# A conformer layer's normed rows in PSUM, its second half's squares on GpSimd, another order of its first projection, and three edits further on

## Chip, cores and metric

The kernel runs on one core of a Trainium2 chip. The metric is device time in microseconds (us) of one execution. All inputs and outputs lie in HBM, in fp32.

## What is computed

A decoder trunk of two layers over 1024 positions of width 1024, cut to what the change touches:

```python
def conformer_conv(u, b_glu, w_dw, b_dw, ln_g, ln_b):
    u = u + b_glu
    a, gate = jnp.split(u, 2, axis=-1)
    v = a * jax.nn.sigmoid(gate)
    v = causal_dwconv(v, w_dw, b_dw)          # width 31, 768 channels
    v = layernorm(v, ln_g, ln_b)
    return jax.nn.silu(v)

# layer 0
h = rmsnorm(x, g_mix[0])
mem_k, mem_v = jnp.split(rmsnorm(mem, g_mem) @ w_mem_kv[0], 2, axis=-1)
p = h @ w_in_a[0]                             # [gate and value | memory queries]
mix = conformer_conv(p[..., :1536], ...)
x = x + concat(mix, memory_attention(p[..., 1536:], mem_k, mem_v)) @ w_out[0]
x = x + conv_ffn(rmsnorm(x, g_ffn[0]), ...)
# layer 1
kvf = rmsnorm(x, g_kv) @ w_kvf                # k, v, 12 forget logits
cum_logf = cumsum(log_sigmoid(kvf[..., 1536:] + b_f))
# queries, forgetting attention with bias cum_logf, memory attention,
# output projection, conv_ffn, final rmsnorm
```

## The kernel before

The sequence lies along the free axis: x is held as eight tiles of 128 channels x 1024 positions, and nearly every step is done for each half of 512 positions (hf 0 and 1). A product in fp32 is made of three fp32r matmuls (lines 108 to 110): each operand is split into a high part, copied by ScalarE (line 81), and a low part, the source minus the high part, on VectorE or GpSimd (line 82). So each tile that TensorE uses needs one copy and one subtract ahead of it.

TensorE, VectorE, ScalarE and GpSimd each run their own queue in order, and wait at an instruction whose operand or buffer isn't ready. A scheduler sets the order within each queue from the order of the program and its own estimates; `issue_after(ins)` holds an instruction behind another one, `later(d)` lowers its priority, and `set_fill` with `drain_fill(n)` doles out a list of steps, n of them at once.

**Start of layer 0** (`layer_a`). `normed(hf)` takes the sum of squares of x over channels (squares on ScalarE, line 152; adds at line 157, and at 159 where two accumulators are joined), sums over partitions with a matmul by ones (line 133), takes the root (line 140, ScalarE) and its reciprocal (line 142, VectorE), and spreads the result over the partitions with four matmuls by the identity (line 123). Those write the first half of the PSUM tile xn (tag b2, two banks). For each of the eight tiles line 801 then makes x * gain * row in an SBUF tile ppre, and line 802 splits it to ah and al. ALO lists the (hf, k) whose subtract runs on GpSimd; TWO = 5 starts a second accumulator for the second half's squares, whose adds run on VectorE. The sum in the first half of positions is psq, in the second nsq. Between these stand the memory's projections mk (line 108 to 110) and mv (line 222) of layer 1 and then layer 0, with the steps on their results, ks and vs.

**Projection and convolution.** The columns of w_in_a come in 128-wide tiles: wia0 to wia5 values (ua), wia6 to wia11 gates (ug), wia12 and 13 memory queries (uq). A step adds two of eight channel tiles for one half. For each channel tile t the order is gate hf 0, gate hf 1, value hf 0, value hf 1, in PSUM banks c0 and c1 by hf. v is value times sigmoid(gate). The depthwise convolution of width 31 is shared out: some taps are diagonal matmuls on TensorE into cpe (lines 108 to 110), some are a ScalarE product ct and a GpSimd add into yp (lines 874 and 875), the rest run on VectorE, in place in cpe for tiles 0 to 4 (line 918). The last tile, v5, is done by half, and its VectorE taps go to an SBUF accumulator (lines 886 and 888) that line 889 adds to yp; line 914 adds yp and cpe. The LayerNorm takes its mean by matmul (line 1014, bank c0 for hf 0, c1 for hf 1) and subtracts it at line 1019. Memory attention runs beside this (ms scores, line 230 and 265 amp, line 276 mt, lines 280 and 281 mo, om its output projection).

**Layer 1** (`layer_b`). The statistics of x are st (line 133) and bc (line 123). The value projection vps (line 1122) takes 24 matmuls for each of eight blocks of 128 positions, three times over, in banks c0 and c1 in turn. Keys and queries (pq) are made by half in bank c0 or c1 and multiplied by the row of the norm into bkc (line 1181) or bqc (line 1183), which sets the bank free. The forget logits are transposed (lft, blf) and summed along the positions by a scan (line 1215, VectorE); line 1218 copies the high part and line 1219 subtracts it. Scores are fs (line 1260).

Of the kernel before, what the change touches and what calls it, by code (L numbers as in the profile page):

```python
# [8 lines left out]
F32 = mybir.dt.float32  # L9
# [3 lines left out]
ALU = mybir.AluOpType  # L13
AX = mybir.AxisListType

P = 128
S = 1024
HS = 512
D = 1024
KD = D // P  # L20
# [31 lines left out]
class Trunk:  # L52
# [668 lines left out]
    def layer_a(self):  # L721
# [14 lines left out]
        with tc.tile_pool(name="pm", bufs=1) as pm:  # L736
# [23 lines left out]
            def ptmp(nm, w=HS):  # L760
                return pm.tile([P, HS], F32, tag="t", name=f"p{nm}", bufs=4)[:, :w]
# [24 lines left out]

            hh, hl = [], []

            def normed(hf):
                xs = [self.x[k][:, hf * HS:(hf + 1) * HS] for k in range(KD)]  # L790
                acc = self.sum_squares(xs, tmp=None if hf else ptmp, eng=nc.gpsimd if hf else nc.vector,
                                       two=self.TWO if hf else None)
                tmp = self.ps.tile([P, 2, HS], F32, tag="b2", name="xn")
                row = self.bcast_row(self.rstd_cols(acc, 4, D, self.eps_rms, tmp[:, 1, :4]), 4, tmp[:, 0])
                hh.append([])
                hl.append([])
                for k in range(KD):
                    hh[hf].append(self.htile(f"ah{hf}{k}"))
                    hl[hf].append(self.htile(f"al{hf}{k}"))
                    t = ptmp("pre")  # L800
                    nc.vector.scalar_tensor_tensor(t, xs[k], self.vec("g_mix0", k), row, op0=ALU.mult, op1=ALU.mult)
                    self.split(hh[hf][k], hl[hf][k], t, lo_eng=nc.gpsimd if (hf, k) in self.ALO else nc.vector)

# [7 lines left out]
            last_bc = self.last_bc.ins  # L811
            normed(0)
            normed(1)
            wv1 = [f(pm2) for f in wv1]
# [7 lines left out]
            self.ps.ring = ("c2", "c3")  # L822
            self.mem_v(mh, ml, rc, vs0, wv0)

            wk0 = [f(pm2) for f in wk0]
            ks0 = tuple(unit([P, NMH, MEM], F32R, f"ks0{i}") for i in range(2))
            self.mem_k(mh, ml, mrb, ks0, wk0)
            self.ps.ring = ("c0", "c1", "c2", "c3")
            nc.sync.dma_start(self.d_ks[0], ks1[0].bitcast(F32))
# [12 lines left out]
        wtl = pb.tile([P, CT * CW], F32R, tag="wtl", name="wtl")  # L842
        self.split(wth, wtl, self.vec("w_dwa", 0, CT * CW))

# [8 lines left out]
        def conv_steps(t):  # L853
# [9 lines left out]
            def start():  # L863
# [12 lines left out]
                if last:  # L876

                    with self.later(self.LATER):
                        d["a"] = []
                        for hf in range(2):  # L880
                            a = self.nt("ca")
                            d["a"].append(a)
                            for j in range(np_, CW):
                                vj = v[:, hf * HS + j:hf * HS + j + HS]
                                if j == np_:
                                    nc.vector.tensor_scalar(a, vj, w(j), None, op0=ALU.mult)
                                else:
                                    nc.vector.scalar_tensor_tensor(a, vj, w(j), a, op0=ALU.mult, op1=ALU.add)
                            nc.vector.tensor_tensor(y[:, hf], y[:, hf], a, op=ALU.add)
# [51 lines left out]
        def glu_steps(t):  # L941
# [3 lines left out]
            def step(i):  # L945
                val, hf, kk = i // 8, i // 4 % 2, i % 4
                j = t if val else CT + t
                if i % 8 == 0:
                    load(j)
                    for j2 in order[order.index(j) + 1:order.index(j) + 2]:  # L950
                        load(j2)
                if kk == 0:
                    d["u"] = self.ps.tile([P, HS], F32, tag=f"c{hf}", name="ua" if val else "ug")
                half(ws[j], d["u"], hf, [2 * kk, 2 * kk + 1])
# [22 lines left out]
        self.set_fill(steps + cv[CT - 1]["taps"], self.ARATE, self.ALAG)  # L977
        self.drain_fill(self.AFIRST)
        memattn(0)
# [65 lines left out]
    def layer_b(self):  # L1045
# [60 lines left out]
        def v_steps(pc_):  # L1106
# [3 lines left out]
            def step(i):  # L1110
# [4 lines left out]
                if kk == 0:  # L1115
                    d["ps"] = self.ps.tile([P, VP], F32, tag=f"c{t % 2}", name="vps")
                ps = d["ps"]
# [47 lines left out]
        def kq_steps(t):  # L1165
# [3 lines left out]
            def step(i):  # L1169
# [9 lines left out]
                if k == KD - 1:  # L1179
                    if n == "k":  # L1180
                        nc.vector.tensor_tensor(d[n][:, sl], d["u"], rb[:, sl], op=ALU.mult)
                    else:
                        nc.vector.scalar_tensor_tensor(d[n][:, sl], d["u"], SCALE, rb[:, sl],
                                                       op0=ALU.mult, op1=ALU.mult)
# [29 lines left out]
        cum = unit([NFOX, S], F32, "cum")  # L1214
        nc.vector.tensor_tensor_scan(cum, on, lf, 0.0, op0=ALU.mult, op1=ALU.add)
        ch = unit([NFOX, S], F32R, "ch")
# [90 lines left out]

        self.drain_fill(self.AHEAD)
        vss = {(0, 0): prep(0, 0), (0, 1): prep(0, 1)}
# [112 lines left out]
    MLAG = 3  # L1422
    ALO = [(0, 3), (0, 4), (0, 6), (1, 1), (1, 3), (1, 4)]
    TWO = 5
    WEARLY = 0
# [154 lines left out]
```

## Time and profile before

| | us |
|---|---|
| median of 3 runs | 2335.38 |
| lowest and highest | 2333.52, 2335.58 |
| the profiled execution's own time | 2334.59 |
| its span on the core | 2332.8 |

The mean granted clock of TensorE was 0.988 of full speed. Times in the rows of the profile are counted from the start of the span. A row of the time line gives start, duration, engine, line, operation, output <- inputs, shape and count; what stands in brackets is the idle time ahead of it and what ended it. A row of the waits gives who waited for whom, the total, how often, and the longest. The rows that the prediction uses are quoted there.

### The profile page before, as it was taken

What the parts mean: (1) busy time and instruction counts of PE and PEld (TensorE: products, weight loads), DVE (VectorE), ACT (ScalarE), POOL (GpSimd) and SP (SyncE); (2) the same over time, 40 slices, a digit from 0 to 9 for tenths busy, and PEclk for the clock granted to TensorE, in tenths of its full rate; (3) what the DMA queues carried; (4) which work ended last, traced back from release to release, by engine and by line L of the source; (5) the groups of instructions that cost most, each with busy time, mean ns of one, the idle gap of its engine ahead of it and who ended that gap; (6) DMA issues with size and microseconds to landing.
All of it is one profiled execution on the core that took longest, in us unless ns stands there. A gap on an engine that the chain in (4) does not pass through costs nothing.

```text
span 2332.8 us, 29689 instructions
## 1 busy us (share of the span) xinstructions
PE 2256.2 (97%) x10970; PEld 1865.7 (80%) x10970; DVE 1460.0 (63%) x1995; ACT 1075.5 (46%) x1864; POOL 1333.7 (57%) x1003
## 2 busy tenths in 40 slices
PE   6999889999999999999998999999999999999998
PEld 6777668878788878888897888788878888778887
DVE  7479787676666664325656777876776666645225
ACT  6776746443434343223542666755444343442212
POOL 3676844666868676453323443614577777766533
PEclk8999989999999999999999999999999999999999
DMA  6100023222222235332332222433222222245322
GB/s 242 37 28 28 29 73 117 72 81 82 82 76 88 78 108 188 106 109 95 123 105 81 71 77 68 124 110 127 67 86 75 81 75 88 79 136 175 112 68 73
DMA packets 85282, 216.74 MB, mean 93 GB/s; under 512 B 9009, under 2 KB 29233, under 8 KB 85137
## 3 DMA queue, kind: packets, MB, share of 16 engines
q1 hardware_dynamic: 84992, 214.52, 28.8%
q8 instruction: 86, 1.41, 0.3%
q14 instruction: 60, 0.48, 0.1%
q10 hardware_dynamic: 144, 0.32, 0.0%
HBM read 156.94 MB, written 51.58 MB: 89 GB/s over the span
## 4 chain that ended last, share of the span: by engine, by line
PE 46%; DVE 3%; POOL 1%; ACT 1%; issue 1%; DMA 0%; DVEq 0%; ACTq 0%; POOLq 0%
PE uY L345 8%; PE uX L345 5%; PE uV L345 5%; PE dn L109 3%; PE dn L108 3%; PE dn L110 3%; PE vps L1122 3%; PE pq L108 2%; PE pq L110 2%; PE pq L109 2%; PE op L108 1%; PE op L109 1%; PE op L110 1%; PE fo L1305 1%; PE fs L1260 1%; PE fo L1304 1%
## 5 line engine op out<-in xcount | busy, mean ns | idle before, releaser
L345 PE MATMUL uY<-fT,fwh 128*128 128x512 f32 x1056 | 331.4, 395 | 4.7 <-DVE fuv L546 3.2
L109 PE MATMUL dn<-gl,wd_hi 128*128 128x512 f32 (+1 forms) x752 | 284.6, 379 | 1.2 <-POOL gl L82 1.2
L108 PE MATMUL dn<-gh,wd_hi 128*128 128x512 f32 (+1 forms) x752 | 280.3, 377 | 0.0
L662 DVE TENSOR_TENSOR fx<-fx,dn 128x512 f32<-128x512 f32 (+1 forms) x176 | 110.9, 636 | 268.8 <-PE dn L110 268.5
L110 PE MATMUL dn<-gh,wd_lo 128*128 128x512 f32 (+1 forms) x752 | 278.9, 375 | 0.0
L345 PEld LDWEIGHTS uY<-fT,fwh 128*128 128x128 f32 x1056 | 196.3, 188 | 55.3 <-DVE fuv L546 9.8
L345 PE MATMUL uX<-fB,fwh 128*128 128x512 f32 x704 | 220.0, 393 | 2.0 <-ACT fuv L521 1.9
L345 PE MATMUL uY<-fT,fwl 128*128 128x512 f32 x528 | 206.6, 391 | 0.0
L82 POOL TENSOR_TENSOR fwl<-wa,fwh 128x512 fp32r<-128x512 f32 x88 | 117.1, 1331 | 137.6 <-ACT fwh L81 137.5
L82 POOL TENSOR_TENSOR wd_lo<-wd_raw,wd_hi 128x1024 fp32r<-128x1024 f32 x44 | 107.9, 2458 | 137.8 <-ACT wd_hi L81 129.0
L108 PEld LDWEIGHTS dn<-gh,wd_hi 128*128 128x128 f32 x752 | 141.2, 188 | 28.3
L109 PEld LDWEIGHTS dn<-gl,wd_hi 128*128 128x128 f32 x752 | 141.3, 188 | 27.0 <-POOL gl L82 2.0
L110 PEld LDWEIGHTS dn<-gh,wd_lo 128*128 128x128 f32 x752 | 141.0, 188 | 27.1
L345 PEld LDWEIGHTS uX<-fB,fwh 128*128 128x128 f32 x704 | 131.6, 188 | 33.3 <-ACT fuv L521 2.8
L82 POOL TENSOR_TENSOR fwl<-wb,fwh 128x512 fp32r<-128x512 f32 x88 | 121.9, 1387 | 63.1 <-ACT fwh L81 60.8
L875 POOL TENSOR_TENSOR yp<-yp,ct 128x512 f32<-128x512 f32 x100 | 135.7, 1359 | 27.6 <-ACT ct L874 22.7
L82 POOL TENSOR_TENSOR gl<-g,gh 128x512 fp32r<-128x512 f32 x88 | 117.5, 1357 | 47.1 <-ACT gh L81 47.1
L345 PE MATMUL uX<-fB,fwl 128*128 128x512 f32 x352 | 137.3, 392 | 0.0
L82 POOL TENSOR_TENSOR fwl<-fs,fwh 128x512 fp32r<-128x512 f32 x88 | 117.8, 1340 | 20.1 <-ACT fwh L81 20.1
L81 ACT CAST fwh<-wa 128x512 fp32r<-128x512 f32 x88 | 54.2, 618 | 140.7 <-PE uY L345 108.3
L81 ACT CAST wd_hi<-wd_raw 128x1024 fp32r<-128x1024 f32 x44 | 45.6, 1050 | 157.6 <-issue 82.2
L345 PEld LDWEIGHTS uY<-fT,fwl 128*128 128x128 f32 x528 | 99.2, 188 | 22.3
(398 smaller groups left out, 6285.4 us busy)
## 6 DMA issues: line engine op xcount, KB each, us to landing
wb<-in_wup SPq DMA_DIRECT2D x44, 512.0 KB
wa<-in_wup SPq DMA_DIRECT2D x44, 512.0 KB
d_g<-fsg SPq DMA_DIRECT2D x44, 512.0 KB
wd_raw<-in_wdn SPq DMA_DIRECT2D x44, 512.0 KB
g<-d_g SPq DMA_DIRECT2D x44, 512.0 KB
d_x<-x SPq DMA_DIRECT2D x32, 256.0 KB
nxs<-d_x SPq DMA_DIRECT2D x32, 256.0 KB
wia_raw<-in_wia SPq DMA_DIRECT2D x14, 512.0 KB
```

The costliest lines, as they stand in the source:

```text
L81: nc.scalar.copy(hi, src)
L82: (lo_eng or nc.gpsimd).tensor_tensor(lo, src, hi.bitcast(F32), op=ALU.subtract)
L108: nc.tensor.matmul(out, lhsT=ah, rhs=bh, start=start and i == 0, stop=False)
L109: nc.tensor.matmul(out, lhsT=ah, rhs=bl, start=False, stop=False)
L110: nc.tensor.matmul(out, lhsT=al, rhs=bh, start=False, stop=stop and i == n - 1)
L345: mm = nc.tensor.matmul(out, lhsT=w[:, k], rhs=h[k], start=start and k == 0 and j == 0, stop=k == n - 1 and j == 2, skip_group_check=True)
L662: return nc.vector.tensor_tensor(self.x[m][:, sl], self.x[m][:, sl], ps, op=ALU.add)
L875: nc.gpsimd.tensor_tensor(y[:, hf], y[:, hf], c, op=ALU.add)
L1122: nc.tensor.matmul(ps, lhsT=a[hf][k][:, tsl], rhs=w[:, k % 4], start=k == 0 and j == 0, stop=k == KD - 1 and j == 2)
L1260: mm = nc.tensor.matmul(o, lhsT=d["q1"][:, qs], rhs=d["k1"][:, ksl], start=True, stop=False)
L1304: nc.tensor.matmul(po, lhsT=vs[:, j], rhs=ph[:, u], start=j == 0, stop=False)
L1305: nc.tensor.matmul(po, lhsT=vs[:, j], rhs=pl[:, u], start=False, stop=j == 2 * I + 1)
```

## The change

Part 1, the start of layer 0. The product x * gain * row goes to the free banks of the two xn tiles, two slots for the first half of positions and three for the second, except for the three tiles whose subtract runs on GpSimd, which keep the SBUF tile. ALO shrinks from six entries to three, TWO goes, so that all seven adds of the second half's squares are GpSimd's. `normed` is cut in two, the statistics and the rows; the memory's value projection of layer 0 is held behind the first half's broadcast, and the second half's rows come after the memory's key projection of layer 0.

Part 2, the projection. For t = 0 the order is gate and value of hf 0, then gate and value of hf 1, and all but two of its first steps are held behind the second half's broadcast.

Part 3, further on: the last tile's accumulator ca lies in PSUM (bank c0 and c1) instead of SBUF; the first two vps tiles use banks c2 and c3; eight steps of keys are issued ahead of the scan, which is held behind the last bkc among them.

```diff
-            def normed(hf):
-                xs = [self.x[k][:, hf * HS:(hf + 1) * HS] for k in range(KD)]
-                acc = self.sum_squares(xs, tmp=None if hf else ptmp, eng=nc.gpsimd if hf else nc.vector,
-                                       two=self.TWO if hf else None)
-                tmp = self.ps.tile([P, 2, HS], F32, tag="b2", name="xn")
-                row = self.bcast_row(self.rstd_cols(acc, 4, D, self.eps_rms, tmp[:, 1, :4]), 4, tmp[:, 0])
+            rows = [self.ps.tile([P, 2, HS], F32, tag="b2", name="xn") for hf in range(2)]
...
+            def squares(hf):
+                return self.sum_squares(xs2[hf], tmp=None if hf else ptmp, eng=nc.gpsimd if hf else nc.vector)
+            def stats(hf):
+                tmp = rows[hf]
+                r = self.rstd_cols(squares(hf), 4, D, self.eps_rms, tmp[:, 1, :4])
+                return self.bcast_row(r, 4, tmp[:, 0])
+            def normed(hf, row):
...
-                    t = ptmp("pre")
+                    if (hf, k) in self.ALO:
+                        t = ptmp("pre")
+                    else:
+                        t = (rows[hf][:, 1], rows[1 - hf][:, 0], rows[0][:, 1])[n % (2 + hf)]
+                        n += 1
                     nc.vector.scalar_tensor_tensor(t, xs[k], self.vec("g_mix0", k), row, op0=ALU.mult, op1=ALU.mult)
-                    self.split(hh[hf][k], hl[hf][k], t, lo_eng=nc.gpsimd if (hf, k) in self.ALO else nc.vector)
+                    e = nc.scalar.copy(hh[hf][k], t)
+                    (nc.gpsimd if (hf, k) in self.ALO else nc.vector).tensor_tensor(
+                        hl[hf][k], t, hh[hf][k].bitcast(F32), op=ALU.subtract)
+                return e.ins
...
-            normed(0)
-            normed(1)
+            row0 = stats(0)
+            bc0 = self.last_bc.ins
+            normed(0, row0)
+            row1 = stats(1)
+            bc1 = self.last_bc.ins
...
-            self.mem_v(mh, ml, rc, vs0, wv0)
-            wk0 = [f(pm2) for f in wk0]
+            with tc.issue_after(bc0):
+                self.mem_v(mh, ml, rc, vs0, wv0)
+                wk0 = [f(pm2) for f in wk0]
...
             self.mem_k(mh, ml, mrb, ks0, wk0)
+            last_ah = normed(1, row1)
...
-        self.split(wth, wtl, self.vec("w_dwa", 0, CT * CW))
+        with self.issue_after(last_ah):
+            self.split(wth, wtl, self.vec("w_dwa", 0, CT * CW))
...
-                            a = self.nt("ca")
+                            a = self.ps.tile([P, HS], F32, tag=f"c{hf}", name="ca")
...
-                val, hf, kk = i // 8, i // 4 % 2, i % 4
+                val, hf, kk = (i // 8, i // 4 % 2, i % 4) if t else (i // 4 % 2, i // 8, i % 4)
...
-                    d["u"] = self.ps.tile([P, HS], F32, tag=f"c{hf}", name="ua" if val else "ug")
+                    d["u"] = self.ps.tile([P, HS], F32, tag=f"c{hf if t else val}", name="ua" if val else "ug")
...
-        self.drain_fill(self.AFIRST)
+        self.drain_fill(2)
+        with self.issue_after(bc1):
+            self.drain_fill(self.AFIRST - 2)
...
-                    d["ps"] = self.ps.tile([P, VP], F32, tag=f"c{t % 2}", name="vps")
+                    d["ps"] = self.ps.tile([P, VP], F32, tag=f"c{t % 2 + 2 * (t < 2 and pc_ == 0)}", name="vps")
...
-                        nc.vector.tensor_tensor(d[n][:, sl], d["u"], rb[:, sl], op=ALU.mult)
+                        self.last_k = nc.vector.tensor_tensor(d[n][:, sl], d["u"], rb[:, sl], op=ALU.mult)
...
-        nc.vector.tensor_tensor_scan(cum, on, lf, 0.0, op0=ALU.mult, op1=ALU.add)
+        self.drain_fill(8)
+        with self.issue_after(self.last_k.ins):
+            nc.vector.tensor_tensor_scan(cum, on, lf, 0.0, op0=ALU.mult, op1=ALU.add)
...
-        self.drain_fill(self.AHEAD)
+        self.drain_fill(self.AHEAD - 8)
...
-    ALO = [(0, 3), (0, 4), (0, 6), (1, 1), (1, 3), (1, 4)]
-    TWO = 5
+    ALO = [(1, 1), (1, 3), (1, 5)]
```

On TensorE's queue, at the start of layer 0, where the first half's statistics (psq) are followed by the 48 mv matmuls of layer 0's memory values:

```order
 L222 MATMUL mv<-mwkl,mh 128x256
 L133 MATMUL xn<-ones_69,psq 128x1 x4
+L123 MATMUL xn<-ident,rs 128x128 x4
 L222 MATMUL mv<-mwwh,mh 128x256
 L222 MATMUL mv<-mwwh,ml 128x256
```

The broadcast (line 123), which stood behind the 48 mv, now stands ahead of them, directly behind the statistics. After them come 2 ug, 24 mk, 7 ug, 24 mk and 3 ug ahead of the second half's statistics, then its broadcast, then 12 ug, 24 ua, 24 uq, 24 uq, 24 ug and 24 ua; on GpSimd four of the seven adds of squares come first, then one wia_lo ahead of each of the other three.

On VectorE's queue at the same place, where rs is the first half's reciprocal, ppre or xn the product and al the low part (line 801 became 814, the subtract of line 82 became 816):

```order
 L142 RECIPROCAL rs<-sd 128x4
-L226 SCALAR_TENSOR_TENSOR vs_542<-mv,rs,vs_542 128x4x64
 L784 CAST maskb<-nmask 128x128
-L226 SCALAR_TENSOR_TENSOR vs_542<-mv,rs,vs_542 128x4x64
-L801 SCALAR_TENSOR_TENSOR ppre<-x_90,vecs,xn 128x512
-L801 SCALAR_TENSOR_TENSOR ppre<-x_91,vecs,xn 128x512
-L801 SCALAR_TENSOR_TENSOR ppre<-x_92,vecs,xn 128x512
-L801 SCALAR_TENSOR_TENSOR ppre<-x_93,vecs,xn 128x512
-L82 TENSOR_TENSOR al_262<-ppre,ah_261 128x512
+L814 SCALAR_TENSOR_TENSOR xn<-x_90,vecs,xn 128x512
+L816 TENSOR_TENSOR al_263<-xn,ah_262 128x512
+L814 SCALAR_TENSOR_TENSOR xn<-x_91,vecs,xn 128x512
```

Products and subtracts of the first half now alternate, since the products have two slots, and the adds of squares that stood among them are gone from this queue.

On VectorE's queue in layer 1, around the scan (printed with operation SCALAR_TENSOR_TENSOR; lines 1211, 1181, 1215 and 1219 became 1234, 1204, 1241 and 1245):

```order
-L1211 COPY blf<-lft 12x512
-L1215 SCALAR_TENSOR_TENSOR bcum<-bon,blf 12x1024
-L1219 TENSOR_TENSOR bcl<-bcum,bch 12x1024
-L1181 TENSOR_TENSOR bkc<-pq,rb 128x512 x2
-L1267 TENSOR_REDUCE nm<-fs 128x1 x2
+L1234 COPY blf<-lft 12x512
+L1204 TENSOR_TENSOR bkc<-pq,rb 128x512
+L1241 SCALAR_TENSOR_TENSOR bcum<-bon,blf 12x1024
+L1245 TENSOR_TENSOR bcl<-bcum,bch 12x1024
+L1204 TENSOR_TENSOR bkc<-pq,rb 128x512
```

The first of the two bkc now stands ahead of the scan. Of the other two edits, the mean matmuls of the convolution's first four tiles (line 1014) leave their places ahead of mt (hf 0) and beside cpe of hf 1, and stand behind cpe of hf 0 and behind the second group of om; and 24 vps stand between st (line 133) and bc (line 123).

More of the change, by code (lines that the diff above doesn't have):

```diff
@@ L787, in layer_a @@
             hh, hl = [], []
-            def normed(hf):
-                xs = [self.x[k][:, hf * HS:(hf + 1) * HS] for k in range(KD)]
-                acc = self.sum_squares(xs, tmp=None if hf else ptmp, eng=nc.gpsimd if hf else nc.vector,
-                                       two=self.TWO if hf else None)
-                tmp = self.ps.tile([P, 2, HS], F32, tag="b2", name="xn")
-                row = self.bcast_row(self.rstd_cols(acc, 4, D, self.eps_rms, tmp[:, 1, :4]), 4, tmp[:, 0])
+            rows = [self.ps.tile([P, 2, HS], F32, tag="b2", name="xn") for hf in range(2)]
+            xs2 = [[self.x[k][:, hf * HS:(hf + 1) * HS] for k in range(KD)] for hf in range(2)]
+            def squares(hf):
[5 more added lines that the diff above has]
+            def normed(hf, row):
+                xs = xs2[hf]
                 hh.append([])
                 hl.append([])
+                n = 0
                 for k in range(KD):
@@ L945, in step @@
             def step(i):
-                val, hf, kk = i // 8, i // 4 % 2, i % 4
+                val, hf, kk = (i // 8, i // 4 % 2, i % 4) if t else (i // 4 % 2, i // 8, i % 4)
                 j = t if val else CT + t
-                if i % 8 == 0:
+                if i % 8 == 0 or (t == 0 and i == 12):
                     load(j)
```

## Prediction

> **What bounds the kernel now.** I read the page's busy shares first, then the list of TensorE's waits, then the stages in which those waits lie.
>
> ```profile
> PE 2256.2 (97%) x10970; PEld 1865.7 (80%) x10970; DVE 1460.0 (63%) x1995; ACT 1075.5 (46%) x1864; POOL 1333.7 (57%) x1003
> ...
> PE mk L108 <- ACT mwwh L81: 10.5, 1, 10.5
> PE pq L108 <- DVE bkc L1181: 6.9, 2, 6.4
> PE cpe L108 <- DVE v L914: 6.3, 1, 6.3
> PE ug L109 <- DVE al L82: 4.7, 2, 3.5
> PE bc L123 <- DVE rs L142: 4.6, 2, 3.6
> ...
> PE xn L133 <- DVE nsq L159: 3.5, 1, 3.5
> ```
>
> TensorE works 2256.2 of the 2332.8 us, and the number of its matmuls does not change, so only the 76.6 us in which it stands, and what it runs at a lower clock, can be won. The first wait (10.5, the program's first load) is not touched. The five others belong to four places that the edits touch: the start of the first layer (ug, xn), the tail of its convolution (cpe), and two places in the second layer (bc, pq).
>
> ```profile
> 40.00:60.00 20.00, 12.99 (x45) 10.01 (x44) 15.10 (x15) 5.65 (x11) 10.97 (x6) 0.66 0.24 79
> 250.00:300.00 50.00, 44.88 (x183) 32.66 (x181) 37.18 (x37) 35.41 (x66) 44.65 (x34) 0.97 0.14 48
> ...
> 1264.08 0.79 PE L108 MATMUL pq<-bh,wk_hi 128*128 128x512 f32 x1 [6.42 <-DVE bkc L1181]
> 1268.02 0.40 PE L108 MATMUL pq<-bh,wk_hi 128*128 128x512 f32 x1
> ```
>
> After the width, the columns are busy PE, PEld, DVE, ACT, POOL, then the granted clock. From 40 to 60 us TensorE is busy 12.99 of 20 at a clock of 0.66: a wait costs its own length and then a slow stretch. Its size shows in the two rows behind: after the wait of 6.42, the nine matmuls from 1264.08 to 1268.02 take 3.94 us, 0.44 each.
>
> **A. The start of the first layer.**
>
> ```profile
> 27.89 0.39 PE L222 MATMUL mv<-mwwh,mh 128*128 128x256 f32 x1
> 33.65 1.05 PE L123 MATMUL xn<-ident,rs 128*128 128x128 f32 x8
> 45.54 0.50 PE L109 MATMUL ug<-al,wia_hi 128*128 128x512 f32 x1 [3.48 <-DVE al L82]
> 51.69 1.87 PE L133 MATMUL xn<-ones,nsq 128*128 128x1 f32 x8 [3.53 <-DVE nsq L159]
> 80.08 0.39 PE L108 MATMUL ua<-ah,wia_hi 128*128 128x512 f32 x1
> 80.31 0.39 PE L109 MATMUL ua<-al,wia_hi 128*128 128x512 f32 x1
> ...
> 32.89 0.18 DVE L142 RECIPROCAL rs<-sd 128x4 f32<-128x4 f32 x1
> 40.96 2.85 DVE L157 TENSOR_TENSOR nsq<-nsq 128x512 f32<-128x512 f32 x1
> 47.77 2.19 DVE L82 TENSOR_TENSOR al<-ppre,ah 128x512 fp32r<-128x512 f32 x1
> 52.97 0.69 DVE L82 TENSOR_TENSOR al<-ppre,ah 128x512 fp32r<-128x512 f32 x1 [0.68 <-ACT ah L81]
> ...
> 34.99 2.68 POOL L157 TENSOR_TENSOR nsq<-nsq 128x512 f32<-128x512 f32 x2 [0.27 <-ACT nsq L152]
> 37.63 5.63 POOL L82 TENSOR_TENSOR wia_lo<-wia_raw,wia_hi 128x1024 fp32r<-128x1024 f32 x2
> ...
> 61.59 1.28 POOL L82 TENSOR_TENSOR al<-ppre,ah 128x512 fp32r<-128x512 f32 x1 [10.51 <-ACT ah L81]
> ...
> L801 DVE SCALAR_TENSOR_TENSOR ppre<-x,vecs,xn 128x512 f32<-128x512 f32 x16 | 11.3, 739 | 4.1 <-PE xn L123 4.0
> ```
>
> A 128x512 matmul starts every 0.23 us when warm (80.08 to 80.31), so the slow stretch costs about 1.9. DVE explains both waits. The same subtract takes 0.69 at 52.97, when POOL is idle (for the 10.51 us before 61.59), and 2.19 at 47.77, when POOL works; an add takes 2.85. All read two SBUF operands. The multiply of line 801, which reads the row from PSUM, averages 0.739 over all 16, half of them beside POOL's work.
>
> The edit moves three adds (40.96 is one) from DVE to POOL and three subtracts the other way, so DVE has 13 subtracts, each with an operand in PSUM. I cost each at 0.7, by row 279.17 below, whose operand mt is in PSUM; the other end is 2.19. Against the edit stands a rule of the Trainium skill, "VectorE: DVE Perf Modes", section "The TRN2 errata": a VectorE instruction has a fixed part of 120 cycles with a PSUM source and 58 with an SBUF source. By it each moved subtract would be some 0.06 us dearer, an estimate of 0.8 us for the 13, most of it off the path. The two rows differ by nothing (0.69 from PSUM, 0.69 from SBUF), so the sum leaves it out.
>
> What it costs first: the broadcast L123 now stands directly behind L133, and everything of TensorE behind L123. The reciprocal that it needs ends at 33.07, and nothing ahead of it on DVE moves. So TensorE stands from 27.8 to 33.1, **5.3 us that before held the 48 mv matmuls**, and restarts cold. The steps: broadcast to 34.9 (the cold one at 1120.69 in C takes 1.68); 48 mv, half as fast until some 3.9 us after 33.1 and then 0.12 each, to 41.6; then 48 mk and 12 ug (48 x 0.12 + 12 x 0.23 = 8.5) to 50.1. The 0.12 is (33.65 - 27.89) / 48. In that time DVE does eight multiplies (0.74) and eight subtracts (0.7), 11.5 us from 35, and with four small steps of 0.45 is through at 48.5; the ug matmuls, which need those subtracts one after another until 55, are not held up. POOL does seven adds and three wia_lo: four adds end at 37.67 as before, then 3 x 2.82 + 3 x 1.34 = 12.5 to 50.2 at the prices of its two rows. So L133 runs at about 50.2 instead of 51.69, and the second broadcast near 52.3 (a wait of 1.0 for its rs, the list's 4.6 less 3.6), with 12 ug (2.8) behind it to 55.1. From there TensorE waits for nothing that I see: 72 x 0.23 = 16.5, to **71.6**, where 96 matmuls of the layer's projection are done, as many as stood before 80.08. Gain 8.5. It carries on, since TensorE hardly waits from there to 200 us. POOL's next wia_lo, now behind four adds of yp, is ready near 81 by the same kind of walk and needed at 71.6 + 48 x 0.23 = 82.6, which is tight. Range 4 to 10.
>
> **B. The tail of the convolution.**
>
> ```profile
> L888 DVE SCALAR_TENSOR_TENSOR nca<-v,vecs,nca 128x512 f32<-128x512 f32 x18 | 19.6, 1091 | 0.2
> L918 DVE SCALAR_TENSOR_TENSOR cpe<-v,vecs,cpe 128x1024 f32<-128x1024 f32 x85 | 108.8, 1282 | 5.1 <-PE cpe L110 3.8
> ...
> 270.17 3.59 PE L1014 MATMUL mean<-v,inv_conv 128*128 128x512 f32 x8
> 279.17 0.69 DVE L279 TENSOR_TENSOR mtl<-mt,mth 128x512 fp32r<-128x512 f32 x1 [3.64 <-ACT mth L278]
> 289.42 1.30 DVE L886 TENSOR_SCALAR nca<-v,vecs 128x512 f32<-128x512 f32 x1
> 299.96 1.35 DVE L889 TENSOR_TENSOR yp<-yp,nca 128x512 f32<-128x512 f32 x1
> 323.95 0.67 DVE L914 TENSOR_TENSOR v<-yp,cpe 128x512 f32<-128x512 f32 x1
> ```
>
> DVE runs almost without a gap from 279 to 324.6, so its work there is the path. L888 reads v and nca, both in SBUF: 1.09 each for 512 columns, where L918 with its accumulator in PSUM takes 1.28 for 1024. At 0.74 (line 801's shape) the second half's nine save 9 x 0.35 = 3.2, its L886 0.6, the two L889 0.65 each: 5.1. The first half's nine lie where DVE then waits 3.64, and save nothing. The four mean matmuls of the first half (3.59) leave their place ahead of mt, on which that wait of 3.64 hangs: 3.6 earlier. They and those of the second half now need the bank that ca holds until L889, so they come after; the second half's 3.6 stands close to the last v, and I charge a third, 1.2. Gain 5.1 + 3.6 - 1.2 = **7.5**. Bounds: 0 if ACT's copies and POOL's adds set the pace, 12 if POOL's own adds get shorter too.
>
> **C. The value projection.**
>
> ```profile
> 1116.13 0.95 PE L133 MATMUL st<-ones,sq 128*128 128x1 f32 x8
> 1120.69 1.68 PE L123 MATMUL bc<-ident,rs 128*128 128x128 f32 x8 [3.62 <-DVE rs L142]
> ...
> 1118.26 0.27 ACT L140 ACTIVATE sd<-st,eps_rms 128x4 f32<-128x4 f32 x1
> ```
>
> 24 vps matmuls now stand in the wait of 3.62. Their bank is that of st, which ACT has read at 1118.53, so 1.47 of the wait stays and 2.15 goes. The broadcast comes when they are done, 1118.55 + 24 x 0.12 = 1121.4, which is 0.7 later, and so do the steps that hang on it; the matmuls behind it are warm, where the broadcast took 1.68 and takes 0.9 to 1.05 warm. Gain 2.15 + 0.7 for the clock, less some 0.35 of the 0.7: **2.5**, range 1 to 4.
>
> **D. The scan.**
>
> ```profile
> 1256.20 0.67 DVE L1211 COPY blf<-lft 12x512 f32<-12x512 f32 x1
> 1256.98 3.68 DVE L1215 TENSOR_TENSOR_SCAN bcum<-bon,blf 12x1024 f32<-12x1024 f32 x1
> 1261.76 1.66 DVE L1219 TENSOR_TENSOR bcl<-bcum,bch 12x1024 fp32r<-12x1024 f32 x1 [1.11 <-ACT bch L1218]
> 1263.35 0.67 DVE L1181 TENSOR_TENSOR bkc<-pq,rb 128x512 f32<-128x512 f32 x1
> ```
>
> bkc frees the bank for the next pq and stood behind scan, ACT's copy and bcl. Now the first bkc runs ahead of the scan, 1257.3 to 1258.0; 24 pq run to 1263.5; scan (3.68), the wait for the copy (1.11) and bcl (1.66) end near 1264.4 and the second bkc at 1265.0. The waits of 6.9 become 0.4 + 1.6 = 2.0, less 4.9; a shorter wait leaves less cold work, some 0.6. The two c transfers leave about 1 us later, beside 24 more pq. Gain **5.5**, range 4 to 6.5.
>
> **The sum.** 8.5 + 7.5 + 2.5 + 5.5 = 24.0 from the profiled execution's 2334.59 (0.8 below the median 2335.38, inside the runs' spread): **2310.6**.
>
> **Rivals.**
> 1. The tail gives nothing. For it: POOL is busy 44.65 of 50 there, and its adds wait for ACT's copies, which the change leaves alone. Against it: DVE has no gap. A + C + D = 16.5: 2318.
> 2. The start gives nothing: the gap of 5.3 and POOL's tight wia_lo near 82 eat the 8.5. For it: the gap is certain, POOL's margin under 2 us. B + C + D = 15.5: 2319.
> 3. PSUM does not spare DVE from POOL. Then each of eight subtracts takes up to 2.19 instead of 0.7, 12 us, A is gone, B keeps 3.6 - 1.2, and B + C + D = 10.4: 2324. Against it: line 801's 0.739, with one SBUF operand, beside POOL. The Trainium skill has the condition in "GPSIMD Engine Reference", section "1. Specifications": POOL shares its SBUF interfaces with VectorE, with contention for VectorE instructions in a 2-port mode or with two SBUF inputs. By that rule the moved subtracts are spared and rival 3 falls; the rows agree as far as they go (0.739 and 0.69 against 2.19).
> 4. Slower. POOL's chain at the start holds TensorE at the second L133, with all the layer's work behind it in order.
>
> ACT's last squares and its three casts of wia_hi now stand between casts of ah, each of which waits for DVE and one of two PSUM slots. If POOL waited 10.5, as it does for ACT ahead of 61.59, at each of its three wia_lo, its last add would end at 50.2 + 31.5 = 81.7: A becomes 31.5 - 8.5 = 23.0 longer, the other 15.5 shorter, and the time is 2342. It decides from a last add at 50.2 + 24.0 = 74.2, which takes 3 us more for each of eight tiles; the one row of such a stall came from a late row, not from slots.
>
> **How the numbers follow.** Forecast 0.60 (2303 to 2317), rival 1 0.16, rival 2 0.12, rival 3 0.06, rival 4 0.06. The bounds of the terms add to gains of 9 to 32.5. Range **2302 to 2325**: rival 4 and the ends of the others stay outside. A measurement of this kernel tells about 0.2% (4.7 us) from no change. Faster: 0.94 from the forecast and rivals 1 to 3, less 0.02 for their own spread; same 0.03, that spread and 0.01 of rival 4; slower 0.05, the rest of rival 4.
>
> **What would show it.** A: a wait of about 5 us before L123 at 33, subtracts of 0.7 beside POOL, L133 near 50, 96 projection matmuls done near 71.5. B: the accumulating steps on ca at 0.74, the last v about 9 us closer to the first. C: vps inside the wait of bc. D: two waits of bkc that sum to about 2. Wrong if the subtracts from PSUM still take over 1 us, if the second L133 comes after 55, if TensorE waits for wia_lo near 82, or if POOL's adds end the tail.

## The result, and the profile after

The changed kernel takes 2313.27 us in the median of four executions (2311.01 to 2317.24), the kernel before 2334.45 beside it: 21.2 us less, a ratio of 0.9911 with a 95% interval of [0.9894, 0.9929]. The forecast was 2310.6, a gain of 24.0 on the profiled execution. The execution profiled after took 2317.24, the slowest of its four, so its rows show 17.4 us of span gained (2332.8 to 2315.4). Two more executions of the same kernel were profiled in the experiments, and they are needed to read it. On the chip of e4 to e7 the executions of the kernel before lay 15 us apart, on that of e11 28, so the kernels there are compared by stages.

The page of after, its list of TensorE's waits, and its stages (the columns as before):

```profile
PE 2251.8 (97%) x10970; PEld 1862.2 (80%) x10970; DVE 1443.2 (62%) x1995; ACT 1075.3 (46%) x1864; POOL 1329.8 (57%) x1003
...
PE xn L123 <- DVE rs L142: 5.9, 2, 5.3
PE mo L281 <- DVE mtl L279: 4.2, 2, 3.9
...
PE cpe L109 <- DVE vl L82: 2.7, 1, 2.7
...
PE pq L108 <- DVE bkc L1204: 1.4, 2, 0.9
...
PE mt L276 <- POOL amp L230: 0.9, 1, 0.9
...
40.00:60.00 20.00, 19.43 (x123) 17.47 (x122) 13.91 (x25) 11.01 (x22) 11.16 (x8) 1.00 0.24 79
250.00:300.00 50.00, 44.54 (x186) 34.21 (x185) 38.33 (x46) 36.42 (x71) 46.03 (x40) 0.92 0.22 80
1250.00:1300.00 50.00, 48.41 (x283) 40.10 (x281) 35.55 (x71) 31.74 (x65) 23.75 (x18) 1.00 0.26 65
```

The waits of ug for al (4.7), of xn for nsq (3.5) and of cpe for v (6.3) are gone; pq's fell from 6.9 to 1.4. The new one, 5.3 ahead of the first broadcast, is the one the prediction charged. From 40 to 60 us TensorE is busy 19.43 of 20 at the full clock, where it was 12.99 at 0.66.

The start, in the time line of after, by engine:

```profile
33.11 2.08 PE L123 MATMUL xn<-ident,rs 128*128 128x128 f32 x8 [5.31 <-DVE rs L142]
49.71 0.95 PE L133 MATMUL xn<-ones,nsq 128*128 128x1 f32 x8
71.91 0.39 PE L108 MATMUL ug<-ah,wia_hi 128*128 128x512 f32 x1
...
45.61 1.28 DVE L816 TENSOR_TENSOR al<-xn,ah 128x512 fp32r<-128x512 f32 x2
...
47.35 1.28 POOL L157 TENSOR_TENSOR nsq<-nsq 128x512 f32<-128x512 f32 x1
```

The statistics of the second half stand at 49.71 (50.2 was worked out), two subtracts from PSUM take 1.28 beside GpSimd's work, and the 97th matmul of the projection starts at 71.91 (71.6 was worked out) instead of 80.08.

The two places in layer 1:

```profile
1109.95 0.39 PE L1145 MATMUL vps<-wv_hi,bh 128*128 128x260 f32 x1 [1.50 <-ACT sd L140]
1114.20 1.33 PE L123 MATMUL bc<-ident,rs 128*128 128x128 f32 x8
...
1246.34 0.69 DVE L1204 TENSOR_TENSOR bkc<-pq,rb 128x512 f32<-128x512 f32 x1 [0.59 <-PE pq L110]
1246.94 2.59 DVE L1241 TENSOR_TENSOR_SCAN bcum<-bon,blf 12x1024 f32<-12x1024 f32 x1
1252.86 0.69 DVE L1204 TENSOR_TENSOR bkc<-pq,rb 128x512 f32<-128x512 f32 x1 [0.56 <-PE pq L110]
```

The vps matmuls stand in the wait, which keeps 1.50 (1.47 was worked out). The first bkc runs ahead of the scan, and the scan takes 2.59 instead of 3.68.

The lead over the kernel before (same instruction, time in the profile of before less time in this one) tells where the time came from. The second column is the first profile, the third a later one of the same kernel (run e10 below):

| at | after | e10 | term |
|---|---|---|---|
| 97th projection matmul, 80.08 before | 8.17 | 7.87 | A: 8.5 |
| ms at 146.13 | 6.10 | 5.86 | |
| first v of the last channel tile, 262.95 | 0.69 | 5.76 | |
| LayerNorm's first broadcast, 344.15 | 9.54 | 16.23 | B: 7.5 |
| first bc of layer 1, 1115.24 | 8.63 | 15.70 | |
| first lft, 1250.14 | 11.12 | 18.53 | C: 2.5 |
| end of the span, 2332.8 | 17.4 | 24.7 | D: 5.5 |

In both, C is 2.5 to 2.8 and D 6.2 to 6.3, of which 5.9 stand at the pq matmul that waited 6.42 before. A is won as forecast and loses 2.0 before 146 us; the first profile loses 5.4 more before 263.

### The profile page after: what moved, and what is told of

The parts are those of the page before. It is cut to its first block, busy times and chain, and to the rows that moved or that the text cites. A ratio compares the mean times of both kernels' runs of the same rounds, so it can differ in the third digit from the quotient of the medians.

```text
span 2315.4 us, 29688 instructions
## 1 busy us (share of the span) xinstructions
PE 2251.8 (97%) x10970; PEld 1862.2 (80%) x10970; DVE 1443.2 (62%) x1995; ACT 1075.3 (46%) x1864; POOL 1329.8 (57%) x1003
## 4 chain that ended last, share of the span: by engine, by line
PE 83%; DVE 5%; POOL 3%; ACT 3%; DMA 3%; issue 2%; SPq 0%; DVEq 0%; POOLq 0%; ACTq 0%
PE uY L345 15%; PE uX L345 10%; PE uV L345 10%; PE dn L109 7%; PE dn L108 7%; PE dn L110 7%; PE vps L1145 3%; PE pq L108 2%; PE pq L110 2%; PE pq L109 2%; PE op L108 2%; PE op L109 2%; PE op L110 2%; POOL yp L896 1%; PE ft L1322 1%
## 5 line engine op out<-in xcount | busy, mean ns | idle before, releaser
L82 POOL TENSOR_TENSOR gl<-g,gh 128x512 fp32r<-128x512 f32 x88 | 117.0, 1352 | 48.7 <-ACT gh L81 48.6
```

The source lines that it names most:

```text
L82: (lo_eng or nc.gpsimd).tensor_tensor(lo, src, hi.bitcast(F32), op=ALU.subtract)
```

## The experiments

Each kernel was timed beside the kernel before on the same chip; ratios are to that. On the chip of e4 to e7, and for e11, the stage times are the surer reading: they are counted from the first half's statistics (the start of xn<-ones,psq) to the 97th matmul of the projection: 53.36 before, 45.16 after. The lag behind after, counted from the same start, is given for 150 to 200 us as well, since it changes at the first mt (93.00 in after) and is steady there. The ratios of e4 to e7 (0.9913 to 0.9927) don't tell these kernels from the changed one (0.9902 to 0.9915), so what their edits cost is shown for the start alone and not for the total.

**e0, the changed kernel again.** No edit.

> The changed kernel unaltered, for a second profile. Its four runs lay between 2311.0 and 2317.2 us, and the profile shown was the slowest of them. Theory 1 (the lead of 8.2 us won at the start is used up ahead of the tail, by VectorE's chain and by TensorE's slow clock after waits): the second profile again shows a lead of at most 4 us at the last tile's first v (262 us in the profile of before), whatever the total. Theory 2 (that loss belongs to the one slow execution): a run near 2311 to 2313 shows a lead of 5 to 6 us there.

2313.48 us, ratio 0.9915 [0.9901, 0.9929]. The lead at the first v is 5.9 (257.02), so the loss of 5.4 belongs to one execution and theory 1 falls in its strict form. But this execution took 2317.99, and for another reason:

```profile
737.58 1.02 ACT L590 ACTIVATE fsg<-y 128x1024 f32<-128x1024 f32 x1 [8.49 <-issue]
...
738.88 1.22 PE L345 MATMUL uY<-fT,fwh 128*128 128x512 f32 x2 [5.77 <-DVE fuv L567]
...
728.33 7.97 DVE L547 TENSOR_TENSOR fuv<-fuv,rb 128x512 f32<-128x512 f32 x1
...
728.24 1.33 POOL L82 TENSOR_TENSOR fwl<-fs,fwh 128x512 fp32r<-128x512 f32 x1
734.46 1.29 POOL L468 TENSOR_TENSOR fs<-wb 128x512 f32<-128x512 f32 x1
735.83 1.59 POOL L469 TENSOR_TENSOR fs<-fs,wa 128x512 f32<-128x512 f32 x1
```

ScalarE stood 8.49 us in the first ConvFFN and TensorE 5.77; that ConvFFN took 8 us longer, the rest was nearly as in e10. The row of VectorE tells why: one product of two SBUF operands, which takes 0.69 at this place in e10, takes 7.97. It starts 0.1 behind the start of one of GpSimd's instructions (728.24), which follow one another without a pause; six of them pass, and it ends at 736.30, soon after GpSimd's first pause (735.75 to 735.83). The steps that ScalarE and TensorE wait for stand behind it on VectorE's queue. Ahead of this line ScalarE's idle time is at most 4.0 in the profiles of before and e10.

**e1, the start alone** (parts 1 and 2; part 3 undone):

```diff
-                            a = self.ps.tile([P, HS], F32, tag=f"c{hf}", name="ca")
+                            a = self.nt("ca")
-                    d["ps"] = self.ps.tile([P, VP], F32, tag=f"c{t % 2 + 2 * (t < 2 and pc_ == 0)}", name="vps")
+                    d["ps"] = self.ps.tile([P, VP], F32, tag=f"c{t % 2}", name="vps")
-        self.drain_fill(8)
-        with self.issue_after(self.last_k.ins):
-            nc.vector.tensor_tensor_scan(cum, on, lf, 0.0, op0=ALU.mult, op1=ALU.add)
+        nc.vector.tensor_tensor_scan(cum, on, lf, 0.0, op0=ALU.mult, op1=ALU.add)
```

> Parts 1 and 2 alone; ca is in SBUF, vps in its old banks, the scan in its old place. Theory 1: the tail takes up nearly all of the lead, so the time is 0 to 4 us below before. Theory 2, and the prediction's term for the start: 6 to 8.5 us below before.

2330.21 against 2334.2: 4.0 us less, ratio 0.9983 [0.9974, 0.9991], at the border between the two theories. Its profile has a lead of 5.95 at the first v, 6.8 at 1900 us, and then, in the second ConvFFN, the same stall (VectorE's product takes 7.95). So the start is worth 4.0 in the median, 6 to 7 where nothing else intervenes.

**e2, ca in PSUM alone** (the kernel before with one line):

```diff
-                            a = self.nt("ca")
+                            a = self.ps.tile([P, HS], F32, tag=f"c{hf}", name="ca")
```

> The kernel before with the last tile's accumulator in PSUM and nothing else. The prediction's term: 7.5 us faster; the profile of the changed kernel gives 8 to 9 between the last tile's first v and the LayerNorm's broadcast. If the tail gains only together with the start's earlier work, under 4.

2324.86: 9.3 us less, ratio 0.9960 [0.9947, 0.9974]. The tail's gain stands on its own and is larger than the term.

**e3, vps and scan alone** (the kernel before with those hunks of the diff).

> The kernel before with the first vps in banks c2 and c3 and with the scan behind the first bkc. The prediction's two terms: 2.5 + 5.5 = 8.0 us faster; the profile of the changed kernel gives 2.5 + 6.3 = 8.8. If TensorE's work in these places were only moved and waited for later, under 4.

2324.85: 9.35 less, ratio 0.9961 [0.9948, 0.9973]. The three together give 4.0 + 9.3 + 9.35 = 22.7, where the whole change gave 20.7 on that chip and 21.2 at first: they add up to within 2 us.

**e4, the products in SBUF** (rest as changed):

```diff
-                    if (hf, k) in self.ALO:
-                        t = ptmp("pre")
-                    else:
-                        t = (rows[hf][:, 1], rows[1 - hf][:, 0], rows[0][:, 1])[n % (2 + hf)]
-                        n += 1
+                    t = ptmp("pre")
```

> The changed kernel with all products x * gain * row back in SBUF tiles, everything else as changed. Theory (a PSUM operand spares VectorE from GpSimd): the first half's subtracts beside the squares' adds average 1.5 to 2.2 us instead of 0.69, the last of them ends near 55 instead of 48.9, TensorE waits in the ug matmuls again, and the 96th projection matmul is done 4 to 8 us later than 71.9. The time is 2 to 8 us above the changed kernel. Rival (the order of the work alone made the gain): subtracts stay near 0.7, the 96th is within 1 us of 71.9.

46.66 to the 97th matmul, 1.5 longer than 45.16, where 4 to 8 were expected. The time line of e4, VectorE and GpSimd:

```profile
37.58 2.73 DVE L812 TENSOR_TENSOR al<-ppre,ah 128x512 fp32r<-128x512 f32 x1
...
49.36 1.75 POOL L157 TENSOR_TENSOR nsq<-nsq 128x512 f32<-128x512 f32 x1
```

The subtracts are slow again as expected (2.73 here, 0.68 to 1.84 for the others ahead of 53 us), and so is GpSimd's add (1.75 against 1.28). But with the adds off VectorE's queue there is slack for it: TensorE waits for no al in its ug matmuls, and its statistics come at 51.16 instead of 49.71. The rest of the price comes later, at the first mt, which waits 0.89 for amp in after and 2.52 here, since GpSimd gets to amp later:

```profile
95.84 1.83 PE L276 MATMUL mt<-ident,amp 128*128 128x128 f32 x4 [2.52 <-POOL amp L230]
```

From 150 to 200 us e4 is 4.5 behind after: the theory's 4 to 8, by another wait than it named. The time is 2323.46 (ratio 0.9927 [0.9902, 0.9951]).

**e5, three adds back on VectorE** (rest as changed):

```diff
-                return self.sum_squares(xs2[hf], tmp=None if hf else ptmp, eng=nc.gpsimd if hf else nc.vector)
+                return self.sum_squares(xs2[hf], tmp=None if hf else ptmp, eng=nc.gpsimd if hf else nc.vector,
+                                        two=5 if hf else None)
```

> The changed kernel with the second accumulator back: three of the seven adds of the second half's squares on VectorE. Theory: those adds have two SBUF operands, take 1.5 to 2.8 us beside GpSimd and stand between the subtracts, so the 96th projection matmul is done 3 to 6 us later than 71.9. Rival (GpSimd's chain of adds, which ends at 48.6, is what holds the statistics): they come earlier, and the 96th matmul is done up to 1 us sooner.

51.34, which is 6.2 longer (5.1 from 150 to 200 us); ratio 0.9914 [0.9889, 0.9939]. Its time line, VectorE and TensorE:

```profile
45.60 2.60 DVE L159 TENSOR_TENSOR nsq<-nsq 128x512 f32<-128x512 f32 x1
...
53.86 1.36 PE L133 MATMUL xn<-ones,nsq 128*128 128x1 f32 x8 [3.23 <-DVE al L817]
```

The add that joins the accumulators takes 2.60 between two subtracts, and the last subtract ends at 53.80. The statistics are released by it: they write into the tile xn whose other bank is one of the two slots, and the last product stands in that slot. So with two slots in xn, the second half's statistics wait for the first half's last subtract, and what delays VectorE there delays all behind.

**e6, the old order of the first tile** (gates of both halves, then values; its three lines of part 2 undone).

> The changed kernel with the old order for the first channel tile (gates of both halves, then values). Theory: after the first 24 ug TensorE needs the second half's rows, of which the first subtract ends near 56 and the last near 68, at once; it waits some 2 to 4 us between 53 and 65 that ua of the first half filled, and its clock drops. The time is 1 to 5 us above the changed kernel. Rival: the memory queries of the first half fill the place, no change.

48.80, 3.6 longer (1.9 from 150 to 200 us); ratio 0.9915 [0.9890, 0.9940]. TensorE then follows the second half's copies and subtracts, as in this row:

```profile
59.41 0.50 PE L109 MATMUL ug<-al,wia_hi 128*128 128x512 f32 x1 [0.86 <-POOL al L816]
```

**e7, 24 of the 48 mv back in the gap** (rest as changed; `mem_v` takes the halves it is to do):

```diff
+            self.mem_v(mh, ml, rc, vs0, wv0, (0,))
             with tc.issue_after(bc0):
-                self.mem_v(mh, ml, rc, vs0, wv0)
+                self.mem_v(mh, ml, rc, vs0, wv0, (1,))
```

> The changed kernel with 24 of the 48 mv matmuls of layer 0 put back ahead of the first broadcast, in the wait of 5.3 us there. If TensorE's own work sets the pace from 33 to 50, 2.9 us of work move into the wait, and the shorter wait of 2.4 us may keep the clock: the second half's statistics come 3 to 4.7 us sooner than 49.7. If GpSimd's last add (done at 48.6) and VectorE's last subtract (48.9) set it, TensorE waits there instead, and the gain at the 96th projection matmul is 0.5 to 1.2 us; the total then moves by less than 2 us.

47.36, which is 2.2 longer rather than shorter (4.6 from 150 to 200 us, where the first mt waits 2.28). The wait ahead of the broadcast falls to 2.10, and this appears instead:

```profile
49.77 1.83 PE L133 MATMUL xn<-ones,nsq 128*128 128x1 f32 x8 [4.40 <-DVE al L816]
```

TensorE is through earlier and waits 4.40 for the others, late, where the slow clock then falls on projection matmuls. The gap of 5.3 us is not lost time that filling would win: the statistics need GpSimd's last add (48.28 + 1.26 here, 47.35 + 1.28 in after) and VectorE's last subtract (48.93 + 0.69 here, 48.21 + 0.69 in after). In after TensorE comes 0.8 behind both and doesn't wait, so that is all that an earlier TensorE could win there. Why both end later in e7 isn't shown.

**e8, the first four amp on VectorE** (rest as changed):

```diff
-        self.nc.gpsimd.tensor_scalar(p, p, r, 1.0, op0=ALU.mult, op1=ALU.mult)
+        self.nsn = getattr(self, "nsn", 0) + 1
+        e = self.nc.vector if self.nsn <= 4 else self.nc.gpsimd
+        e.tensor_scalar(p, p, r, 1.0, op0=ALU.mult, op1=ALU.mult)
```

> The changed kernel with the first four normalisations of memory weights (amp) on VectorE instead of GpSimd, where they stand behind adds of yp and a wia_lo. Theory: of the lead of 8.2 us at the 96th projection matmul, 2.0 are lost at the first mt, which waits 0.9 for amp and then takes 1.69 instead of 0.60; with amp on VectorE, idle for two thirds of that stretch, that wait goes and the lead at the ms matmul of 140.03 is 7.5 to 8.2 instead of 6.1. The total is 1 to 2 us below the changed kernel. Rival: the next wait takes its place (mtl, or wia_lo), the lead stays near 6.

It aimed at where the lead of 8.2 falls to 6.1. In the time line of after, GpSimd and TensorE:

```profile
92.46 1.85 POOL L230 TENSOR_SCALAR amp<-amp,r 128x256 f32<-128x256 f32 x4
...
93.00 1.69 PE L276 MATMUL mt<-ident,amp 128*128 128x128 f32 x4 [0.89 <-POOL amp L230]
```

The four mt wait 0.89 and take 1.69, since each follows one of GpSimd's four amp, 0.46 apart; without a wait they take 0.60: 0.89 + 1.09 = 2.0, all of the fall. In e8 the same place reads:

```profile
93.06 0.30 PE L278 MATMUL mt<-ident,amp 128*128 128x128 f32 x1 [0.67 <-DVE amp L232]
94.30 1.00 PE L278 MATMUL mt<-ident,amp 128*128 128x128 f32 x3 [0.95 <-DVE amp L232]
```

Two waits instead of one, and the lead at 146.13 is 4.3 instead of 5.9 to 6.1: the theory fails, and the result is worse than the rival's. 2315.01 (ratio 0.9916 [0.9902, 0.9929]), above e10's 2311.82 beside it. That the loss is at this mt is shown by the rows; a cure was not found.

**e9, the means held back, ca in SBUF** (the kernel before with a PSUM bank kept from the first tap to the last add):

```diff
                             a = self.nt("ca")
+                            b = self.ps.tile([P, HS], F32, tag=f"c{hf}", name="hold")
...
                                     nc.vector.tensor_scalar(a, vj, w(j), None, op0=ALU.mult)
+                                    nc.vector.tensor_copy(b[:, :1], a[:, :1])
...
                             nc.vector.tensor_tensor(y[:, hf], y[:, hf], a, op=ALU.add)
+                            nc.vector.tensor_copy(a[:, :1], b[:, :1])
```

> The kernel before with the accumulator left in SBUF, but with a PSUM bank of its kind held from its first step until it is added to yp (two one-column copies for each half), so that the mean matmuls have to move as they did in the change. It parts the tail's term: PSUM operand 5.1, means moved 3.6 - 1.2 = 2.4. If both are right this kernel is about 2 us faster than before, and the rest of the 9.3 that the accumulator in PSUM brought is the operand's. If the moved means alone bring 6 or more, the operand is worth little; if this kernel is slower than before, the means cost more than they give and the operand brings over 9.

2338.01 against 2333.98: 4.0 us slower, ratio 1.0016 [1.0007, 1.0025]. The profile is 3.9 longer than that of before: 1.4 ahead of the tail, 1.7 in it, 0.7 behind. To read the term, the tail is cut into three stretches, at the first mtl (the low part of mt) and at the last v. In before the last tile's first v starts at 262.95; the rows of its mtl (279.17) and last v (323.95) stand in the prediction. VectorE in after (first v 262.26), then in e9 (first v 264.36):

```profile
270.88 0.69 DVE L279 TENSOR_TENSOR mtl<-mt,mth 128x512 fp32r<-128x512 f32 x1 [0.29 <-ACT mth L278]
310.47 0.68 DVE L935 TENSOR_TENSOR v<-yp,cpe 128x512 f32<-128x512 f32 x1
...
L909 DVE SCALAR_TENSOR_TENSOR ca<-v,vecs,ca 128x512 f32<-128x512 f32 x18 | 13.5, 749 | 0.2
```

```profile
276.88 0.69 DVE L279 TENSOR_TENSOR mtl<-mt,mth 128x512 fp32r<-128x512 f32 x1 [0.61 <-ACT mth L278]
300.24 1.74 DVE L891 TENSOR_TENSOR yp<-yp,nca 128x512 f32<-128x512 f32 x1
305.37 0.15 DVE L892 COPY nca<-hold 128x1 f32<-128x1 f32 x1
324.15 0.68 DVE L917 TENSOR_TENSOR v<-yp,cpe 128x512 f32<-128x512 f32 x1
```

| gain against before, us | predicted | e9 | after | e10 |
|---|---|---|---|---|
| first v to first mtl (16.2 before) | 3.6 | 3.7 | 7.6 | 7.6 |
| first mtl to last v (44.8) | 5.1 | -2.5 | 5.2 | 5.1 |
| last v to the output projection's matmul at 399.89 (75.9) | -1.2 | -2.9 | -3.4 | -1.7 |
| together | 7.5 | -1.7 | 9.4 | 11.0 |

The steps on ca take 0.75 instead of 1.09. In the first stretch the moved means bring 3.7, as worked out, and VectorE's wait falls from 3.64 to 0.61. With ca in PSUM as well it is 7.6: once the wait is gone, the first half's nine steps stand on the path, and their saving counts. In the second stretch e9 loses, by a wait of TensorE. TensorE, then GpSimd in e9 and in after:

```profile
305.57 2.07 PE L1017 MATMUL mean<-v,inv_conv 128*128 128x512 f32 x2 [5.27 <-DVE nca L892]
...
293.52 14.38 POOL L875 TENSOR_TENSOR yp<-yp,ct 128x512 f32<-128x512 f32 x9
```

```profile
285.81 12.09 POOL L896 TENSOR_TENSOR yp<-yp,ct 128x512 f32<-128x512 f32 x9
```

Held, the means make TensorE wait 5.27 for the bank; in after they wait for none. But 3.5 of the 5.27 is e9's own: its copy, which sets the bank free, stands behind other work and ends at 305.52, while the add that needs the accumulator ended at 301.98. So e9 overstates what the held bank costs, and the price of the moved means and the worth of the operand beyond the first stretch aren't parted. GpSimd's nine adds take 1.60 each beside an accumulator in SBUF and 1.34 beside one in PSUM; over all 28 adds of the tail it is 1.42 before, 1.47 in e9 and 1.29 in after. The operand frees both engines.

**e10, the changed kernel a third time**, beside e8 and e9.

> The changed kernel again, beside these two on one chip: 20 to 21 us below before.

2311.82: 22.2 us less, ratio 0.9902 [0.9888, 0.9915]. Its profiled execution took 2309.95 with a span of 2308.1, 24.7 below the profile of before. What parts it from the first profile begins at one instruction. First e10 (TensorE, then VectorE), then after:

```profile
204.37 0.38 PE L259 MATMUL ms<-aks,amq 128*128 128x256 f32 x1 [2.63 <-ACT amp L265]
204.94 0.40 PE L108 MATMUL ug<-ah,wia_hi 128*128 128x512 f32 x1
...
237.23 2.39 DVE L82 TENSOR_TENSOR vl<-v,vh 128x1054 fp32r<-128x1054 f32 x1
```

```profile
204.06 0.58 PE L259 MATMUL ms<-aks,amq 128*128 128x256 f32 x1 [2.62 <-ACT amp L265]
205.08 0.63 PE L108 MATMUL ug<-ah,wia_hi 128*128 128x512 f32 x1
...
239.74 3.64 DVE L82 TENSOR_TENSOR vl<-v,vh 128x1054 fp32r<-128x1054 f32 x1
245.22 0.79 PE L281 MATMUL mo<-mtl,vs 128*128 128x512 f32 x1 [3.93 <-DVE mtl L279]
```

The same wait, 2.63 and 2.62. In e10 the clock stays up (a matmul takes 0.40, and one starts every 0.23); in after the twelve ug take 0.63 and start every 0.43. By the order of the rows, TensorE's delay then puts vl, a subtract of two SBUF operands, beside more of GpSimd's work (3.64 instead of 2.39), so mtl is late, the next wait is 3.93, and a second slow stretch follows: the clock is 0.66 from 244 to 254 us, where it is 0.97 in e10. That is the 5.1 us between the two columns at 262.95. The chain is read from these rows; no run tests it.

**e11, the seven adds on GpSimd alone** (the kernel before with `two=None`).

> The kernel before with all seven adds of the second half's squares on GpSimd, and nothing else changed. Undoing this in the changed kernel cost 6.2 us at the 96th projection matmul. If the adds are worth that by themselves, the 96th matmul is done near 74 instead of 80.08. If they pay only together with the rest (three subtracts and a wia_lo taken off GpSimd's queue ahead of the last add, other work for TensorE meanwhile), GpSimd's last add ends near 55, TensorE waits for it at the statistics instead of 51.7, and the 96th matmul is done between 78.5 and 82; the time is then within 2 us of before.

53.39 to the 97th matmul, as before (53.36); ratio 0.9994 [0.9971, 1.0017]. In its time line:

```profile
52.87 1.27 POOL L157 TENSOR_TENSOR nsq<-nsq 128x512 f32<-128x512 f32 x1
...
54.20 1.05 PE L133 MATMUL xn<-ones,nsq 128*128 128x1 f32 x8 [0.58 <-POOL nsq L157]
```

GpSimd's last add ends at 54.1, behind three subtracts of its own. The adds pay only with the shorter ALO and the other order.

## Why the prediction was right, and where it wasn't

**The sum** was 24.0; the medians gained 21.2, 20.7 and 22.2. The 24.7 of e10's span is that of the fastest of the changed kernel's twelve executions. The likeliest case came, and the range held the time, but that the sum is this near is in part luck: A keeps about 2.5 less than was forecast and the tail gives 2 to 3.5 more.

**A, the start (8.5).** The steps hold to 0.5 us: gap 5.3 (5.31), statistics at 50.2 (49.71), 96 matmuls done at 71.6 (71.91), subtracts of 0.7 (0.67 to 0.69). What failed is the size of what is kept, at "It carries on, since TensorE hardly waits from there to 200 us". The prediction looked along GpSimd's queue for wia_lo, which came in time, and not for amp behind it: 2.0 are lost there in after, e0, e1 and e10, and 5.9 to 6.1 are kept. Alone the part is worth 4.0 in the median (e1), about half of the term. The explanation within A was too simple, not false. By "DVE explains both waits" the PSUM operand should have counted; without it (e4) 1.5 of the 8.2 are gone at the 97th matmul and 4.5 of the 6.1 behind the first mt. But undoing the adds costs 6.2 and 5.1 at these two places (e5), the order 3.6 and 1.9 (e6), and the adds alone bring nothing (e11). The parts share one slack and don't add.

**B, the tail (7.5).** Right in direction, 9.3 alone (e2), 9.4 to 11.0 by the stages. The moved means' 3.6 came (3.7 in e9), and so nearly did the second half's 5.1 (5.1 and 5.2; in e1, whose tail has before's code, this stretch is 2.1 shorter and the next 1.3 longer than in before, so the agreement isn't closer than that). The step that failed is "The first half's nine lie where DVE then waits 3.64, and save nothing": the same paragraph takes that wait away, and then they save 3.9 (7.6 - 3.7). The charge of 1.2 for the means behind the last v was too small (1.7 and 3.4). GpSimd's adds get shorter as the upper bound of 12 allowed; what that is worth by itself isn't shown.

**C (2.5) and D (5.5).** C is 2.5 and 2.8, 3.3 in e0. D is 5.9 at the pq matmul of 1264.08, in e0 and e3 as well, and 5.3 (e0) to 6.3 by the end of the span. Together they give 9.35 alone (e3). The scan takes 2.59 instead of 3.68, which the prediction left at 3.68. The neighbour that sets this is GpSimd's q, in before and in after:

```profile
1252.37 6.14 POOL L1236 TENSOR_TENSOR q<-bqc,q 64x1024 fp32r<-64x1024 f32 x2 [0.80 <-DVE q L1234]
```

```profile
1241.24 6.15 POOL L1262 TENSOR_TENSOR q<-bqc,q 64x1024 fp32r<-64x1024 f32 x2 [1.07 <-DVE q L1260]
```

These end at 1258.51 and 1247.39, and the scan, which reads two SBUF operands, ends 2.14 later both times: 1260.65 and 1249.53. In all fourteen profiles it ends 2.14 or 2.15 behind GpSimd's q, whether it starts 1.53 ahead of that, as in before, or some 0.45, as in after.

**The rivals.** The first fell by e2. The second is half true: 2.0 of A go to GpSimd's queue and more to the clock in some executions; filling half of the gap won nothing (e7). The third fell: in after the moved subtracts take 0.69 beside GpSimd's work, by the condition that the Trainium skill gives in "GPSIMD Engine Reference", section "1. Specifications"; e4, with two SBUF operands, has one at 2.73. The rule held against the change ("VectorE: DVE Perf Modes", section "The TRN2 errata": a longer fixed part from PSUM) isn't seen: 0.69 from PSUM, as from SBUF. The fourth didn't come: GpSimd's last add of squares ended at 48.6.

## What to carry to other kernels

Where VectorE and GpSimd work at the same time, an accumulator or a product that VectorE rereads is worth a free PSUM bank: it shortens GpSimd's instructions too, so count both. When an edit takes a wait away, count the work that the wait had hidden. A lead won at one stage counts only up to the next wait of each engine that feeds the bound one, so walk every queue to the stage's end and not only the transfer that looks tight, and read what an edit costs behind that wait (e4: 1.5 ahead of it, 4.5 behind). Filling a visible gap on the bound engine wins nothing while the engines that feed it set the pace; it moves the wait to a place where the slow clock may cost more.

## What the hardware showed beyond that

Equal waits of TensorE had unequal prices. After 2.62 and 2.63 us one execution ran the next twelve matmuls at 0.43 us each and the other at 0.23. "TensorE: Matmul & The Clock Gate" of the Trainium skill, Part 1, describes half the clock after idle time; these rows show that near this length the outcome differs between executions of one kernel, and that it can set off a second wait, 5 us in all.

A VectorE instruction with two SBUF operands can be held far longer than it runs. The product that takes 0.69 in e10 takes 7.95 to 7.97 once in six of the fourteen profiles (e0, e1, e4, e5, e6 and e11, which has before's code but for the adds). Each time it starts up to 0.1 behind a GpSimd instruction, six of these pass without a pause, and it ends 0.55 behind the start of the first pause, of 0.08. In e10 both engines' instructions start at 709.22, VectorE's takes 0.69 and GpSimd's 1.84 instead of 1.3. In e0 that ConvFFN took 8 us longer. The scan is alike on a smaller scale: it ends 2.14 behind GpSimd's instruction, however early it started. Both are read from the rows; no run changes GpSimd's work there.
